# Powers of a diagonal state-space layer at half width, with the input side's table in PSUM and its products on VectorE

## The chip, the core and the metric

One core of a Trainium2 chip runs the kernel. The metric is the device time of one execution in microseconds. The engines have a queue each: TensorE (PE, matrix products), VectorE (DVE) and GpSimd (POOL) for elementwise work, ScalarE (ACT, activations and copies), and SyncE (SP), which starts the transfers. DVE, ACT and POOL read and write SBUF; PE writes PSUM, DVE and ACT read and write it too.

## The reference

The trunk maps x, one sequence of 512 rows with 1024 columns in fp32, to the same shape: an S5 state-space layer, an MLP, a dilated attention layer that reads shared keys and values, another MLP, and a last norm. Each sub-layer is an RMS norm, a shift and scale from a conditioning vector, the mixer, a gate and a residual sum. Only the state-space mixer is touched:

```python
lam_bar = jnp.exp(lam * dt)
b_bar = ((lam_bar - 1.0) / lam)[..., None] * b_mat
bu = jnp.einsum('bsgc,gpc->bsgp', ug, b_bar)
a = jnp.broadcast_to(lam_bar, (1, seq) + lam_bar.shape)
_, state = lax.associative_scan(combine, (a, bu), axis=1)
y = jnp.einsum('bsgp,gcp->bsgc', state, c_mat).real.reshape(bsz, seq, dm)
y = y + d_skip.astype(f32) * uf
z = jax.nn.gelu(y).astype(u.dtype)
val, gate = jnp.split(z @ w_glu, 2, axis=-1)
return val * jax.nn.sigmoid(gate)
```

Here `lam_bar` is a complex number for each of 64 groups and 64 states; a group has 16 input and 16 output columns.

## The kernel before

The state-space layer works in chunks of 8 steps. The 64 groups are cut into four units, `ft` = 0 to 3, and a unit into two halves, `s` = 0 and 1, of 8 groups. `ssm_powers` builds the powers of lambda by doubling, each step a complex product of six instructions (`cmul`, L352 to L357): those for b (`pcr`, `pci`) on DVE, those for c (`pwr`, `pwi`) on POOL. They are 64 groups wide on all 128 partitions (real and imaginary rows, 64 each), each with all groups.

For every unit and half, `ssm_p` makes P, powers times `bT`, by two products and a sum of 128x1024 (L562, L563, L564). `ssm_p_tr` transposes P on PE (L575), and ACT copies the result out of PSUM (L576). `ssm_q` on POOL makes Q, powers times c (L590 to L592), and small parts (L601 to L607) from which PE makes the kernel K inside a chunk (L623 to L629, copied by ACT in L642). `ssm_in_tr` turns x (L327), `ssm_in` scales and shifts it (L347, L348, or L342 on ACT). `ssm_d` multiplies it by the turned P (L665), giving each chunk's state. `ssm_scan` turns the states by the rotation angles and runs the scan on DVE (L681 to L704). `ssm_out` gives y of the unit (L718, L722, copied by ACT in L724), and `ssm_out_tr` turns it (L738), applies Gelu (L741) and casts it (L744). The GLU's matrix products are L827 to L829; their fp32 weights are split before into two parts by L799 and L801 on ACT, DVE and POOL.

Ahead of all this `norm_x` sums the squares of x on ACT (L203) and takes the root (L208); DVE makes the reciprocal `rs` (L1610), with which ACT scales x (L215). The rotation angles come from DVE (L528 to L530) and ACT (L536 to L539). `ada_steps` are the gate's parts (PE L1578, DVE L1582 and L1585).

PE, ACT, DVE and POOL run the block in the order in which `ssm` is written (the work of `ssm_params` ahead of the powers is scheduled freely). Tiles of PSUM come from two rings of four, `mm` and `aux`, of one 512-element bank each; a tile can be written when the one four places ahead of it in its ring has been read.

Of the kernel before, what the change touches and what calls it, by code (L numbers as in the profile page):

```python
# [94 lines left out]
class Trunk:  # L95
# [469 lines left out]

    def ssm_p_tr(self, ft, s):
# [5 lines left out]
        for hb in (2 * s, 2 * s + 1):  # L572
            pt = self.aux_ps().rearrange("p (g x) -> p g x", g=4)
            for j in range(4):
                nc.tensor.transpose(pt[:, j], u["pp"][:, hb * 4 + j].rearrange("p l c -> p (l c)"), self.ident)  # L575
            nc.scalar.copy(u["pT"][:, hb * 4:hb * 4 + 4], pt)  # L576

    def ssm_q(self, ft, eng):
# [16 lines left out]
        for s in range(2):
            g = s * GI + ft * 8
            g8 = slice(s * 8, s * 8 + 8)
            b8 = bz[:, 0:512].rearrange("p (g x) -> p g x", x=32)[:, g8, 16:32]
            tb = fl[:, 896:1024].rearrange("p (g c) -> p g c", c=16)
            c0 = [self.pw[4 + i][:, g:g + 8].unsqueeze(2).broadcast_to([P, 8, 16]) for i in range(2)]  # L600
            eng.tensor_tensor(b8, c0[0], self.bT[:, 0, g:g + 8], ALU.mult)  # L601
            eng.tensor_tensor(tb, c0[1], self.bT[:, 1, g:g + 8], ALU.mult)
            eng.tensor_tensor(b8, b8, tb, ALU.add)
# [1 line left out]
        for s in range(2):
            g = s * GI + ft * 8
            eng.tensor_tensor(dk[:, s * 8:s * 8 + 8], self.dT[:, g:g + 8].unsqueeze(2).broadcast_to([32, 8, 32]),  # L607
                              self.cst[0:32, C_DK:C_DK + 32].unsqueeze(1).broadcast_to([32, 8, 32]), ALU.mult)

# [1174 lines left out]
```

## Time and profile before

| what | value |
|---|---|
| time, median of three runs | 1554.1 us (1552.74 to 1558.91) |
| profiled execution | 1553.38 us, its span 1551.6 us |
| PE | busy for 1460.4 us, 94% of the span |
| DVE | 943.8 us, 61% |
| ACT | 569.1 us, 37% |
| POOL | 134.1 us, 9% |
| granted clock of PE, mean | 0.98 |

The span is the time from the first to the last instruction of the profiled execution, and the 1.8 us between it and that execution's own time lie around it. A busy share is an average over the whole span: PE's 94% are made of stretches with nearly all of it and of a beginning with much less.

### The profile page before, as it was taken

The numbers are of one execution on the slowest core, as the hardware profiler recorded it, in microseconds if no ns is written. First come the engines' busy times: TensorE is split into PE (matmuls) and PEld (weight loads), VectorE is DVE, ScalarE is ACT, GpSimd is POOL, SyncE is SP. The second block draws the span as 40 slices with busy tenths as digits, with TensorE's granted clock in tenths as the row PEclk, the third lists the DMA queues.
The fourth block names the chain that finished last, engine by engine and source line by source line (L and its number), as shares of the span: only waits on it lengthen the run. The fifth ranks groups of instructions, "written<-read, shape, count | busy, mean of one in ns | idle before, by whom it ended". The sixth has DMA issues, their size and how long they took to land.

```text
span 1551.6 us, 27063 instructions
## 1 busy us (share of the span) xinstructions
PE 1460.4 (94%) x11540; PEld 1224.5 (79%) x11540; DVE 943.8 (61%) x1641; ACT 569.1 (37%) x989; POOL 134.1 (9%) x112
## 2 busy tenths in 40 slices
PE   2666999999999999999999999999999999999998
PEld 1445789888888888987987888898779888888887
DVE  8999996889984345626646756533558434344322
ACT  5556633423242233522323322332435413232222
POOL 8867100000000000100000000000000000000000
PEclk9788999999999999999999999999999999999999
DMA  9413580976643333233444445222324233232301
GB/s 225 140 56 83 163 245 28 309 233 213 205 151 109 109 99 111 65 99 116 137 130 137 144 115 151 83 56 72 122 83 136 82 109 105 85 109 82 109 1 55
DMA packets 214488, 188.59 MB, mean 122 GB/s; under 512 B 7480, under 2 KB 208352, under 8 KB 214368
## 3 DMA queue, kind: packets, MB, share of 16 engines
q1 hardware_dynamic: 214368, 186.87, 39.5%
q8 instruction: 90, 1.47, 0.4%
q14 instruction: 30, 0.25, 0.1%
HBM read 182.66 MB, written 4.19 MB: 120 GB/s over the span
## 4 chain that ended last, share of the span: by engine, by line
PE 82%; DVE 12%; DMA 2%; issue 2%; ACT 1%; SPq 0%; POOL 0%; DVEq 0%; ACTq 0%
PE mm L827 22%; PE mm L828 22%; PE mm L829 22%; PE mm L1253 2%; PE mm L1254 2%; PE mm L1255 2%; DVE W L801 1%; PE mm L1170 1%; DMA h<-in_ada_w_dram 1%; PE aux L1107 1%; PE aux L1142 1%; PE mm L1163 1%; DVE W L563 1%; PE aux L1115 1%; DVE aacc L1495 1%
## 5 line engine op out<-in xcount | busy, mean ns | idle before, releaser
L799 ACT CAST W<-W 128x1024 fp32r<-128x1024 f32 (+1 forms) x228 | 223.7, 1031 | 392.2 <-PE mm L828 202.0
L827 PE MATMUL mm<-uz,W 128*128 128x512 f32 (+1 forms) x952 | 360.2, 381 | 2.9 <-DVE h L1385 2.7
L829 PE MATMUL mm<-uz,W 128*128 128x512 f32 (+1 forms) x952 | 358.6, 377 | 3.0 <-DVE W L801 3.0
L828 PE MATMUL mm<-uz,W 128*128 128x512 f32 (+1 forms) x952 | 358.3, 377 | 2.5 <-DVE uz L749 2.1
L801 DVE TENSOR_TENSOR W<-W,W 128x1024 fp32r<-128x1024 f32 (+1 forms) x228 | 266.3, 1196 | 148.3 <-ACT W L799 123.1
L827 PE MATMUL mm<-hid,W 128*128 128x512 f32 (+1 forms) x792 | 298.5, 378 | 0.6 <-ACT W L1277 0.3
L828 PE MATMUL mm<-hid,W 128*128 128x512 f32 (+1 forms) x792 | 296.1, 374 | 2.7 <-DVE hid L1001 2.7
L829 PE MATMUL mm<-hid,W 128*128 128x512 f32 (+1 forms) x792 | 295.5, 373 | 0.0
L827 PEld LDWEIGHTS mm<-uz,W 128*128 128x128 f32 x952 | 180.1, 189 | 36.9 <-DVE h L1385 2.8
L829 PEld LDWEIGHTS mm<-uz,W 128*128 128x128 f32 x952 | 180.2, 189 | 35.9 <-DVE W L801 3.4
L828 PEld LDWEIGHTS mm<-uz,W 128*128 128x128 f32 x952 | 180.1, 189 | 34.6 <-DVE uz L749 2.6
L828 PEld LDWEIGHTS mm<-hid,W 128*128 128x128 f32 x792 | 149.2, 188 | 29.4 <-DVE hid L1001 3.8
L827 PEld LDWEIGHTS mm<-hid,W 128*128 128x128 f32 x792 | 148.8, 188 | 28.4 <-issue 1.4
L829 PEld LDWEIGHTS mm<-hid,W 128*128 128x128 f32 x792 | 149.0, 188 | 26.5
L852 DVE SCALAR_TENSOR_TENSOR h<-mm,ada,h 128x512 f32<-128x512 f32 (+1 forms) x77 | 54.1, 707 | 150.7 <-PE mm L829 150.6
L1495 DVE SCALAR_TENSOR_TENSOR aacc<-W,cs,aacc 128x256 f32<-128x256 f32 x196 | 95.3, 486 | 4.0
L1029 DVE TENSOR_TENSOR sg<-sg 128x512 f32<-128x512 f32 x64 | 43.7, 687 | 56.4 <-ACT uz L1028 56.2
L1027 ACT ACTIVATE sg<-mm 128x512 f32<-128x512 f32 x60 | 35.6, 595 | 115.5 <-PE mm L829 114.0
L1253 PE MATMUL mm<-W,hid 128*128 128x256 f32 x256 | 73.5, 287 | 0.0
L1254 PE MATMUL mm<-W,hid 128*128 128x256 f32 x256 | 72.4, 283 | 0.0
L1255 PE MATMUL mm<-W,hid 128*128 128x256 f32 x256 | 72.4, 283 | 0.0
L1126 ACT ACTIVATE sg<-aux,st 128x192 f32<-128x192 f32 (+3 forms) x64 | 36.7, 577 | 95.4 <-DVE st L1124 95.4
(329 smaller groups left out, 1694.5 us busy)
## 6 DMA issues: line engine op xcount, KB each, us to landing
W<-in_mlp_w_dram SPq DMA_DIRECT2D x64, 1024.0 KB, 5.4
W<-in_ada_w_dram SPq DMA_DIRECT2D x20, 1024.0 KB, 7.3
h<-in_ada_w_dram SPq DMA_DIRECT2D x64, 256.0 KB, 3.1
W<-in_w_kv_dram SPq DMA_DIRECT2D x12, 1024.0 KB, 5.3
W<-in_w_kv_dram SPq DMA_DIRECT2D x24, 512.0 KB, 4.3
W<-in_attn_w_q_dram SPq DMA_DIRECT2D x24, 512.0 KB, 5.9
W<-in_ssm_w_glu_dram SPq DMA_DIRECT2D x16, 512.0 KB, 5.4
W<-in_kv_ada_w_dram SPq DMA_DIRECT2D x8, 1024.0 KB, 5.5
```

The costliest lines, as they stand in the source:

```text
L799: h = (nc.gpsimd.tensor_copy if first else nc.scalar.copy)(wh[:, ks], raw[:, ks])
L801: j = eng.tensor_tensor(wl[:, ks], raw[:, ks], wh[:, ks].bitcast(F32), ALU.subtract)
L827: nc.tensor.matmul(o, wh[:, k], uh, start=(start and k == order[0]), stop=False)
L828: nc.tensor.matmul(o, wh[:, k], ul, start=False, stop=False)
L829: self.pe_mark = nc.tensor.matmul(o, wl[:, k], uh, start=False, stop=(stop and k == order[-1])).ins
L852: self.mark = nc.vector.scalar_tensor_tensor(self.h[k][:, cs], src[:, cs], gate[:, k:k + 1], self.h[k][:, cs], ALU.mult, ALU.add).ins
L1029: nc.vector.tensor_tensor(rl, rl, rl, ALU.mult)
L1126: self.act_mark = nc.scalar.activation(p[:, 0:W], ps[:, 0:W], AF.Exp, bias=st[:, 1, e:e + 1], scale=0.125, accum_out=st[:, 2, e:e + 1]).ins
L1253: nc.tensor.matmul(ps[:, j], us[0], wh, start=(k == 0), stop=False)
L1254: nc.tensor.matmul(ps[:, j], us[0], wl, start=False, stop=False)
L1255: nc.tensor.matmul(ps[:, j], us[1], wh, start=False, stop=(k == KT - 1))
L1495: i = nc.vector.scalar_tensor_tensor(acc, raw[k], self.cs[:, k:k + 1], acc, ALU.mult, ALU.add)
```

## The change

The q vectors (lambda, its eighth power's angle and size, and the factor of b) are no longer doubled. Twelve small products with the identity (`by_set`) put the two halves of the groups on two sets of 64 partitions, so the powers are 32 wide instead of 64 on the same 128 partitions. DVE's 24 instructions of `cmul` fall from 64, 64, 128 and 256 elements to half of that, and POOL's 18 from 64, 128 and 192.

From there the powers are spread out again by ACT. Those for c go to an SBUF table by four copies of 64x512. Those for b go to a tile of PSUM, `pcu`, which is held for the whole block: `ssm_pc(ft)` copies one unit's part with eight copies of 64x64, into one of two halves of the tile in turn. It is called for unit 0 in `ssm_powers` and for the others ahead of their P.

P is made on DVE alone. Its products read `pcu`. The products of P(1,1) leave POOL, and P(2,1) is no longer divided between DVE and POOL. For units 0 and 1 the sum is not made on DVE: PE adds the two products, with two products by the identity into the same part of PSUM in place of one transpose. Units 2 and 3 keep sum and transpose. In `ssm_q` three instructions take the place of six, and one the place of two. The reciprocal `rs` moves ahead of P(0,0). `d0` and `d1`, two tiles of the `aux` ring before, share one. Lines behind L417 have other numbers than before.

```diff
+    def by_set(self, out, x):
+
+        for s in range(2):
+            rows = slice(s * GI, s * GI + GI)
+            self.nc.tensor.matmul(out[s * 64:s * 64 + 64], x[rows], self.ident[rows, rows], start=True, stop=True,
+                                  tile_position=(s * GI, s * 64))
+
...
-        G = 64
+        G = GI
...
-            nc.tensor.transpose(pt[:, i], q[:, i].rearrange("g s n -> g (s n)"), self.ident[0:G, 0:G])
-        pw = self.w([P, 4, 8, G])
-        pwr, pwi, pcr, pci = [pw[:, i] for i in range(4)]
-        t1, t2, t3, t4 = [qx[:, 16 + 4 * i:20 + 4 * i] for i in range(4)]
+            self.by_set(pt[:, i], q[:, i])
+
+        pw = self.w([P, 48, G])
+        self.pw = pw[:, 0:32].rearrange("p (i l s) g -> p i l s g", i=2, s=2)
+        pcr, pci = self.pc = [pw[:, 32 + 8 * i:40 + 8 * i] for i in range(2)]
+        pws = qx[:, 0:8].rearrange("p x (y g) -> p (x y) g", y=2).rearrange("p (i l) g -> p i l g", i=2)
+        pwr, pwi = pws[:, 0], pws[:, 1]
+        t1, t2, t3, t4 = [qx[:, 16 + 4 * i:20 + 4 * i, 0:G] for i in range(4)]
...
-        self.pw = (pwr, pwi, pcr, pci, pc0[:, 0], pc0[:, 1])
+        self.pcu = self.aux_ps().rearrange("p (b x) -> p b x", b=2)
+        self.ssm_pc(0)
+        for c in range(2):
+            for s in range(2):
+                nc.scalar.copy(self.pw[c * 64:c * 64 + 64, :, :, s], pws[s * 64:s * 64 + 64])
+
+    def ssm_pc(self, ft):
+
+        pc = self.pcu[:, ft % 2].rearrange("p (i l s g) -> p i l s g", i=2, s=2, g=8)
+        for c in range(2):
+            for s in range(2):
+                for i in range(2):
+                    self.nc.scalar.copy(pc[c * 64:c * 64 + 64, i, :, s],
+                                        self.pc[i][s * 64:s * 64 + 64, :, ft * 8:ft * 8 + 8])
 
     def ssm_turns(self):
 
@@ -539,8 +558,12 @@
         act(er, er, AF.Sin, scale=-TWO_PI, bias=self.half_pi)
 
     def pw4(self, i, ft, s, n):
-        g = s * GI + ft * 8
-        return self.pw[i][:, 0:n, g:g + 8].rearrange("p l g -> p g l").unsqueeze(3).broadcast_to([P, 8, n, 16])
+        g = slice(ft * 8, ft * 8 + 8)
+        if i < 2:
+            x = self.pw[:, i, 0:n, s, g]
+        else:
+            x = self.pcu[:, ft % 2].rearrange("p (i l s g) -> p i l s g", i=2, s=2, g=8)[:, i - 2, 0:n, s]
+        return x.rearrange("p l g -> p g l").unsqueeze(3).broadcast_to([P, 8, n, 16])
...
-            pp, tp = u["pp"][:, s * 8 + g.start:s * 8 + g.stop], tz[:, g]
-            pr, pi, b1, b2 = [x[:, g] for x in (self.pw4(2, ft, s, 8), self.pw4(3, ft, s, 8),
-                                               self.ch4(self.bT, 0, ft, s, 8), self.ch4(self.bT, 1, ft, s, 8))]
-            eng.tensor_tensor(pp, pr, b1, ALU.mult)
-            eng.tensor_tensor(tp, pi, b2, ALU.mult)
+        pp = u["pp"][:, s * 8:s * 8 + 8]
+        tp = u["zs"][:, 2 * s:2 * s + 2].rearrange("p i g c -> p (i g c)").rearrange("p (g l c) -> p g l c", g=8, c=16)
+        eng.tensor_tensor(pp, self.pw4(2, ft, s, 8), self.ch4(self.bT, 0, ft, s, 8), ALU.mult)
+        eng.tensor_tensor(tp, self.pw4(3, ft, s, 8), self.ch4(self.bT, 1, ft, s, 8), ALU.mult)
+        u["p", s] = [pp]
+        if ft < 2:
+            u["p", s].append(tp)
+        else:
             eng.tensor_tensor(pp, pp, tp, ALU.add)
 
     def ssm_p_tr(self, ft, s):
@@ -572,7 +596,12 @@
         for hb in (2 * s, 2 * s + 1):
             pt = self.aux_ps().rearrange("p (g x) -> p g x", g=4)
             for j in range(4):
-                nc.tensor.transpose(pt[:, j], u["pp"][:, hb * 4 + j].rearrange("p l c -> p (l c)"), self.ident)
+                xs = [x[:, hb % 2 * 4 + j].rearrange("p l c -> p (l c)") for x in u["p", s]]
+                if len(xs) == 1:
+                    nc.tensor.transpose(pt[:, j], xs[0], self.ident)
+                    continue
+                for k, x in enumerate(xs):
+                    nc.tensor.matmul(pt[:, j], x, self.ident, start=(k == 0), stop=(k == 1))
             nc.scalar.copy(u["pT"][:, hb * 4:hb * 4 + 4], pt)
...
+        c0 = [self.pw[:, i, 7, :, g].unsqueeze(3).broadcast_to([P, 2, 8, 16]) for i in range(2)]
+        bs = [self.bT[:, i].rearrange("p (s g) c -> p s g c", s=2)[:, :, g] for i in range(2)]
+        eng.tensor_tensor(b8, c0[0], bs[0], ALU.mult)
+        eng.tensor_tensor(tb, c0[1], bs[1], ALU.mult)
+        eng.tensor_tensor(b8, b8, tb, ALU.add)
...
-        d0, d1 = self.aux_ps(), self.aux_ps()
+        d01 = self.aux_ps()
+        d0, d1 = d01[:, 0:P], d01[:, P:]
...
+        self.nc.vector.reciprocal(self.rs, self.rs)
         self.ssm_p(0, 0, dve)
-        self.nc.vector.reciprocal(self.rs, self.rs)
         self.scale_x(0)
...
         self.ssm_p_tiles(1)
-        self.ssm_p(1, 1, pool)
+        self.ssm_pc(1)
+        self.ssm_p(1, 1, dve)
         self.ssm_q(1, pool)
...
         self.ssm_p_tiles(2)
+        self.ssm_pc(2)
         self.ssm_p(2, 0, dve)
...
-        self.ssm_p(2, 1, dve, pool)
+        self.ssm_p(2, 1, dve)
         self.ssm_q(3, pool)
...
         self.ssm_p_tiles(3)
+        self.ssm_pc(3)
         self.ssm_p(3, 0, dve)
         self.ssm_p_tr(3, 0)
         self.some(steps, 1)
```

In `order` rows, the number behind a name tells tiles of one name apart, and xN stands for N instructions in a row. First DVE's queue at the end of the powers, where `rs` is the norm's reciprocal and `W_365`, `W_366` are the products of P of unit 0. Before:

```order
L562 TENSOR_TENSOR W_365<-W_290,W_156 128x1024
L563 TENSOR_TENSOR W_366<-W_290,W_156 128x1024
L564 TENSOR_TENSOR W_365<-W_365,W_366 128x1024
L1610 RECIPROCAL rs_363<-rs_363 128x8
L528 TENSOR_TENSOR hid_468<-cst_63,rq_294 128x2048
L529 TENSOR_SCALAR hid_469<-hid_468 128x2048
L530 SCALAR_TENSOR_TENSOR hid_468<-hid_469,hid_468 128x2048
L293 TENSOR_TENSOR sg_473<-aux_281,cst_63 128x128
```

After, with `W_382` and `W_383` as these products and `aux_343` as `pcu`:

```order
L357 TENSOR_TENSOR W_295<-W_295,W_121 128x128
L1638 RECIPROCAL rs_380<-rs_380 128x8
L582 TENSOR_TENSOR W_382<-aux_343,W_156 128x1024
L583 TENSOR_TENSOR W_383<-aux_343,W_156 128x1024
L547 TENSOR_TENSOR hid_488<-cst_63,rq_299 128x2048
L548 TENSOR_SCALAR hid_489<-hid_488 128x2048
L549 SCALAR_TENSOR_TENSOR hid_488<-hid_489,hid_488 128x2048
L293 TENSOR_TENSOR sg_493<-aux_281,cst_63 128x128
L295 TENSOR_REDUCE red_89_495<-sg_493 128x8
L305 TENSOR_TENSOR redb_91_501<-red_89_495,cst_63 128x16 x2
```

The reciprocal, which reads ACT's square root, has moved ahead of P(0,0) and the three rotation steps, and P's sum is gone.

Next DVE's queue between the modulation of unit 0 (L314) and scan(0), after the change (the one before has L347 in place of the first two rows of `W_568` and `W_569`, which are P of unit 1):

```order
L314 COPY mod_92_505<-aux_497 128x48
L315 SCALAR_TENSOR_TENSOR mod_92_505<-mod_92_505 128x16
L681 MEMSET sqs_512 128x8
L582 TENSOR_TENSOR W_568<-aux_343,W_156 128x1024
L583 TENSOR_TENSOR W_569<-aux_343,W_156 128x1024
L347 TENSOR_TENSOR W_384<-mm_478,mod_92_505 128x512
L348 TENSOR_TENSOR W_384<-W_384,mod_92_505 128x512
L347 TENSOR_TENSOR W_384<-mm_483,mod_92_505 128x512
L348 TENSOR_TENSOR W_384<-W_384,mod_92_505 128x512
```

Two rows of P(1,1) now stand ahead of the input of unit 0 (L347).

ACT's queue at the end of the b and c copies, before:

```order
L478 COPY W_157<-aux_195 64x64x8 x2
L203 ACTIVATE sqs_340,ss_339<-hid_93 128x512 x4
L178 COPY vcol_65_347<-aux_345 128x64
L178 COPY vcol_67_351<-aux_349 128x96
L237 COPY dT_355<-aux_353 32x64
```

and after, L537 being `ssm_pc(0)` and L529 the copies of the powers for c:

```order
L475 COPY W_157<-aux_195 64x64x8 x2
L537 COPY aux_343<-W_295 64x8x8 x8
L529 COPY W_295<-W_121 64x16x32 x4
L203 ACTIVATE sqs_357,ss_356<-hid_93 128x512 x4
L178 COPY vcol_65_364<-aux_362 128x64
L178 COPY vcol_67_368<-aux_366 128x96
```

Twelve copies have come ahead of the norm's squares.

Last, ACT's queue at `ssm_out_tr(0)` and the y copies of out(1), before:

```order
L741 ACTIVATE W_367<-aux_1117 128x4x64 x2
L741 ACTIVATE W_367<-aux_1124 128x4x64 x2
L744 CAST uz_170_1131<-W_367 128x512 x2
L724 COPY W_542<-aux_1170 128x8x64
L724 COPY W_542<-aux_1188 128x8x64
L576 COPY W_1211<-aux_1212 128x512
L576 COPY W_1211<-aux_1218 128x512
```

and after (L769 and L772 are L741 and L744 before, L752 is L724, L605 is L576):

```order
L670 COPY W_111<-aux_1045 32x4x32 x4
L769 ACTIVATE W_384<-aux_1159 128x4x64 x2
L769 ACTIVATE W_384<-aux_1166 128x4x64 x2
L772 CAST uz_170_1173<-W_384 128x512 x2
L752 COPY W_569<-aux_1212 128x8x64
L752 COPY W_569<-aux_1230 128x8x64
L537 COPY aux_343<-W_295 64x8x8 x8
L605 COPY W_1261<-aux_1262 128x512
```

The eight copies of `ssm_pc(3)`, which P(3,0) reads, stand behind the two y copies of out(1).

## Rows read from the trace of the kernel before

**Rows 1.** View by windows: stretch, length, busy time and count per engine, clock, DMA.
```profile
120.00:166.00 46.00, 36.25 (x532) 30.43 (x532) 45.38 (x52) 37.25 (x89) 28.31 (x20) 0.86 0.34 93
150.00:166.00 16.00, 12.51 (x102) 9.83 (x100) 15.72 (x22) 15.72 (x37) 6.88 (x5) 0.89 0.47 133
166.00:175.00 9.00, 7.41 (x60) 6.32 (x62) 8.79 (x17) 3.61 (x9) 0.00 (x0) 0.81 0.85 231
175.00:340.00 165.00, 165.00 (x914) 142.37 (x911) 138.26 (x264) 63.92 (x95) 2.72 (x2) 1.00 0.65 199
```

**Rows 2.** Chain that ended last, 0 to 180 us: start, length, what.
```profile
43.24 7.12 DVE hid L530
...
70.49 3.65 PE aux L575 x16
```

**Rows 3.** Timeline of DVE from 14 to 36 us: start, length, instruction, [idle before].
```profile
15.71 0.35 DVE L353 TENSOR_TENSOR W<-W 128x64 f32<-128x64 f32 x1
...
20.68 0.68 DVE L353 TENSOR_TENSOR W<-W 128x128 f32<-128x128 f32 x1
...
22.46 1.88 DVE L356 TENSOR_TENSOR W<-W,W 128x128 f32<-128x128 f32 x1
...
35.25 1.42 DVE L562 TENSOR_TENSOR W<-W,W 128x1024 f32<-128x1024 f32 x1
```

**Rows 4.** Timeline of POOL in the same stretch.
```profile
22.36 1.84 POOL L590 TENSOR_TENSOR uz<-W,W 128x896 f32<-128x896 f32 x1
```

**Rows 5.** Timeline of ACT, 8 to 56 us.
```profile
18.20 0.63 ACT L203 ACTIVATE sqs<-hid 128x512 f32<-128x512 f32 x1
...
23.57 0.59 ACT L178 COPY vcol<-aux 128x64 f32<-128x64 f32 x2 [2.39 <-PE aux L176]
...
28.54 0.27 ACT L208 ACTIVATE rs<-aux,eps 128x8 f32<-128x8 f32 x1
39.55 3.30 ACT L215 ACTIVATE W<-hid,rs 128x256 f32<-128x256 f32 x8 [10.74 <-DVE rs L1610]
...
44.18 0.48 ACT L251 COPY lam<-aux 32x64 f32<-32x64 f32 x3 [1.14 <-PE aux L247]
```

**Rows 6.** Timeline of DVE, 36 to 137 us.
```profile
55.00 2.81 DVE L564 TENSOR_TENSOR W<-W,W 128x1024 f32<-128x1024 f32 x1
...
61.72 3.15 DVE L562 TENSOR_TENSOR W<-W,W 128x1024 f32<-128x1024 f32 x1
...
84.82 1.22 DVE L562 TENSOR_TENSOR W<-W,W 128x1024 f32<-128x1024 f32 x1
...
94.58 0.68 DVE L685 TENSOR_TENSOR sg<-mm,hid 128x512 f32<-128x512 f32 x1
95.18 1.98 DVE L686 TENSOR_TENSOR W<-W,sg 128x512 f32<-128x512 f32 x1
...
122.25 2.82 DVE L562 TENSOR_TENSOR W<-W,W 128x1024 f32<-128x1024 f32 x1
...
136.68 0.68 DVE L681 TENSOR_TENSOR W<-mm,hid 128x512 f32<-128x512 f32 x1
```

**Rows 7.** Timeline of POOL, 88 to 125 us.
```profile
94.51 2.09 POOL L592 TENSOR_TENSOR uz<-uz,hid 128x896 f32<-128x896 f32 x1
```

**Rows 8.** Timeline of ACT, 56 to 137 us.
```profile
58.67 1.07 ACT L576 COPY W<-aux 128x512 f32<-128x512 f32 x2 [6.37 <-PE aux L575]
...
68.09 0.20 ACT L859 ACTIVATE scrap<-eps 128x1 f32<-128x1 f32 x1
...
76.04 7.69 ACT L229 COPY h<-mm 128x256 f32<-128x256 f32 x16 [1.28 <-PE mm L226]
...
127.99 2.03 ACT L741 ACTIVATE W<-aux 128x256 f32<-128x256 f32 x4
```

**Rows 9.** Timeline of PE, 126 to 182 us.
```profile
131.35 0.69 PE L718 MATMUL aux<-W,W 128*64 128x128 f32 x4 [5.95 <-DVE sg L1582]
...
167.59 0.79 PE L829 MATMUL mm<-uz,W 128*128 128x512 f32 x1 [2.96 <-DVE W L801]
```

More of the change, by code (lines that the diff above doesn't have):

```diff
@@ L413, in ssm_params @@
         qx = self.w([P, 32, G])
-        q = qx[0:G, 0:12].rearrange("p (i j) n -> p i j n", j=2)
+        q = qx[0:G, 0:6]
         (LR, LI, Y8, R8, CR, CI) = [q[:, i] for i in range(6)]
@@ L417, in ssm_params @@
         (RD, TH, X0, X1, X2, X3, RR, C0, S0, X4) = [x[:, i] for i in range(10)]
-        def two(y):
-            return y.unsqueeze(1).broadcast_to([G, 2, G])
         v.tensor_scalar(RD, lre, ld, None, ALU.mult)
@@ L423, in ssm_params @@
         nc.scalar.activation(RR, RD, AF.Exp)
-        nc.scalar.activation(R8, two(RD), AF.Exp, scale=float(L))
+        nc.scalar.activation(R8, RD, AF.Exp, scale=float(L))
         v.tensor_scalar(X0, TH, 1.0 / (2.0 * math.pi), MAGIC, ALU.mult, ALU.add)
@@ L437, in ssm_params @@
         v.scalar_tensor_tensor(X0, X4, -PI_4_2, X0, ALU.mult, ALU.add)
-        v.tensor_scalar(Y8, two(X0), 4.0 / math.pi, None, ALU.mult)
+        v.tensor_scalar(Y8, X0, 4.0 / math.pi, None, ALU.mult)
         v.tensor_tensor(X2, lre, lre, ALU.mult)
@@ L445, in ssm_params @@
         v.tensor_scalar(C0, X1, -2.0, 1.0, ALU.mult, ALU.add)
-        v.tensor_tensor(LR, two(RR), two(C0), ALU.mult)
-        v.tensor_tensor(LI, two(RR), two(S0), ALU.mult)
-        l1, l2 = LR[:, 0], LI[:, 0]
+        v.tensor_tensor(LR, RR, C0, ALU.mult)
+        v.tensor_tensor(LI, RR, S0, ALU.mult)
+        l1, l2 = LR, LI
         v.tensor_scalar(X0, l1, -1.0, None, ALU.add)
@@ L453, in ssm_params @@
         v.tensor_tensor(X1, X1, X3, ALU.add)
-        v.tensor_tensor(CR, two(X1), two(X2), ALU.mult)
+        v.tensor_tensor(CR, X1, X2, ALU.mult)
         v.tensor_tensor(X1, l2, lre, ALU.mult)
@@ L457, in ssm_params @@
         v.tensor_tensor(X1, X1, X3, ALU.subtract)
-        v.tensor_tensor(CI, two(X1), two(X2), ALU.mult)
+        v.tensor_tensor(CI, X1, X2, ALU.mult)
         bc = [self.w([P, 2, G, 16]) for _ in range(2)]
@@ L488, in ssm_powers @@
         pool = nc.gpsimd
-        G = 64
+        G = GI
         q, qx = self.q, self.qx
-        pt = self.aux_ps().rearrange("p (i g) -> p i g", g=G)
+        pt = self.aux_ps()[:, 0:6 * G].rearrange("p (i g) -> p i g", g=G)
         for i in range(6):
-            nc.tensor.transpose(pt[:, i], q[:, i].rearrange("g s n -> g (s n)"), self.ident[0:G, 0:G])
-        pw = self.w([P, 4, 8, G])
-        pwr, pwi, pcr, pci = [pw[:, i] for i in range(4)]
-        t1, t2, t3, t4 = [qx[:, 16 + 4 * i:20 + 4 * i] for i in range(4)]
+            self.by_set(pt[:, i], q[:, i])
[5 more added lines that the diff above has]
+        t1, t2, t3, t4 = [qx[:, 16 + 4 * i:20 + 4 * i, 0:G] for i in range(4)]
         v.tensor_copy(pwr[:, 0], pt[:, 0])
         v.tensor_copy(pwi[:, 0], pt[:, 1])
-        pc0 = pw[:, 0:2, 7]
+        pc0 = pws[:, :, 7]
         v.tensor_copy(pc0, pt[:, 4:6])
         rq = self.t([P, 2, GI], "rq")
-        for s in range(2):
-            rows = slice(s * 64, s * 64 + 64)
-            v.tensor_copy(rq[rows], pt[rows, 2:4, s * GI:(s + 1) * GI])
+        v.tensor_copy(rq, pt[:, 2:4])
         self.y8, self.r8 = rq[:, 0], rq[:, 1]
@@ L552, in ssm_p_tiles, with ssm_p @@
         u["zs"] = self.w([P, 4, 8, NC])
-    def ssm_p(self, ft, s, eng, eng2=None):
+    def ssm_p(self, ft, s, eng):
         u = self.unit[ft]
-        tz = u["zs"][:, 2 * s:2 * s + 2].rearrange("p i g c -> p (i g c)").rearrange("p (g l c) -> p g l c", g=8, c=16)
-        for eng, g in ((eng, slice(0, 5)), (eng2, slice(5, 8))) if eng2 else ((eng, slice(0, 8)),):
-            pp, tp = u["pp"][:, s * 8 + g.start:s * 8 + g.stop], tz[:, g]
-            pr, pi, b1, b2 = [x[:, g] for x in (self.pw4(2, ft, s, 8), self.pw4(3, ft, s, 8),
-                                               self.ch4(self.bT, 0, ft, s, 8), self.ch4(self.bT, 1, ft, s, 8))]
-            eng.tensor_tensor(pp, pr, b1, ALU.mult)
-            eng.tensor_tensor(tp, pi, b2, ALU.mult)
+        pp = u["pp"][:, s * 8:s * 8 + 8]
[6 more added lines that the diff above has]
+        else:
             eng.tensor_tensor(pp, pp, tp, ALU.add)
@@ L594, in ssm_q @@
         bz = u["bz"] = self.bz[ft % 2]
[L595 to L603, printed above, removed]
+        b8 = bz[:, 0:512].rearrange("p (s g x) -> p s g x", s=2, x=32)[:, :, :, 16:32]
+        tb = fl[:, 0:256].rearrange("p (s g c) -> p s g c", s=2, c=16)
+        g = slice(ft * 8, ft * 8 + 8)
+        c0 = [self.pw[:, i, 7, :, g].unsqueeze(3).broadcast_to([P, 2, 8, 16]) for i in range(2)]
[3 more added lines that the diff above has]
+        eng.tensor_tensor(b8, b8, tb, ALU.add)
         dk = u["dk"] = self.t([32, 16, 32], "rstd", 2)
[L605 to L608, printed above, removed]
+        d = self.dT.rearrange("p (s f j) -> p f s j", s=2, j=8)[:, ft]
+        eng.tensor_tensor(dk.rearrange("p (s j) x -> p s j x", s=2), d.unsqueeze(3).broadcast_to([32, 2, 8, 32]),
+                          self.cst[0:32, C_DK:C_DK + 32].unsqueeze(1).unsqueeze(1).broadcast_to([32, 2, 8, 32]),
+                          ALU.mult)
     def ssm_k(self, ft):
```

## The prediction, before the changed kernel ran

> **What bounds the kernel now.** I read the view by windows first. From 175 us on TensorE (PE) is busy in every microsecond and the clock is at its upper level [rows 1]; VectorE (DVE) is the second there, at 138 of 165 us. The change touches nothing in that part, so it can act only by moving the moment at which PE becomes saturated. Ahead of 175 us PE has gaps: 9.8 us between 120 and 166, 1.6 us between 166 and 175, at clocks of 0.86 and 0.81 [rows 1], while DVE is busy for 45.4 of 46 us. So I read the chain next: through the SSM block it runs nearly without break over DVE, with a few pieces of PE and ACT. Two of its pieces matter later: the rotation's last step, 7.12 us for one instruction, and the transposes of P(1,0) and P(1,1), 3.65 us for 16 [rows 2]. The last long gap of PE is at 167.59, behind a weight split on DVE that stands after the last scan [rows 9]. What the change is worth is therefore the time at which DVE finishes its four scans, less what PE can fill in.
>
> Why is DVE slow? The timelines show instructions that wait, not work. A 128x128 product of the powers takes 0.68 us, and 1.88 us when a 128x896 product of POOL begins 0.1 us ahead of it [rows 3, 4]. The products of P take 1.22 us each with POOL idle, 2.81 to 3.15 us beside it [rows 6]. A DVE instruction with one operand in PSUM does not wait: 0.68 us at 94.58, while the very next one, with two SBUF operands, needs 1.98 us, both beside POOL's 2.09 us [rows 6, 7].
>
> **The change, step by step**, on the clock of the profiled execution.
>
> 1. *Powers.* DVE's 24 products become 32, 32, 64 and 128 wide. From the starts in [rows 3] a 64-wide one costs 0.28 us and a 128-wide one about 0.6; with 0.25 for 32: 12 x 0.25 + 6 x 0.35 + 6 x 0.55 = 8.4 at most, about 7 where POOL is out of the way. POOL's first Q product now waits for ACT's copies of the powers, which stand behind the end of the powers, so nothing of POOL but its own narrow powers runs beside them. From 15.5 that ends at 22 to 24 (22.7 taken), against 35.25 [rows 3]: **-12.5**.
> 2. *ACT's queue.* The eight copies of pc(0) and four of the powers stand ahead of the norm's squares (the order rows show it). For an ACT copy of 64 elements the nearest rows are 0.48/3 = 0.16 us (64 elements) and, above it, 3.30/8 = 0.41 (256 elements) [rows 5]; I take 0.2, near the first, so 1.6 for eight, from 1.3 to 3.3. The four wide ones are like L178's 0.59 [rows 5]: 2.4. Thus 22.7 + 1.6 + 2.4 = 26.7. The squares up to the square root took 18.20 to 28.81, with 2.39 of it waiting [rows 5]: 8.2 of work. So rs is ready at 34.9. Before, it was ready at 28.8 and nobody on DVE waited. The reciprocal now stands ahead of P(0,0), so P(0,0), two rotation steps and all behind wait for it: **+12.5**, and P(0,0) starts at 35 as before. Scaling x starts at 35.2 instead of 39.55 [rows 5].
> 3. *P(0,0), rotation, P(0,1).* Two products instead of three, 2.4 instead of 4.1. POOL has only Q(0) from about 27 to 41 and no P, so the rotation's last step costs about 2.4 (twice a 1024-wide product) instead of 7.12; P(0,1) costs 2.4 instead of the 5.2 that end at 57.8 [rows 6]. Sum -1.7 - 4.7 - 2.8 = -9.2: DVE is through P(0,1) at about 48.
> 4. *P(1,1) moves to DVE, ahead of the first input product,* and reads pc(1). Its copies stand in ACT's queue behind P_tr(0,1)'s copies, which waited for PE until 58.67, the rotation's Abs and Sin, the scaling of x and a table load, which ran without a gap from 58.67 to 68.29 [rows 8]: 9.6 us. P_tr(0,1) has 32 instructions of 0.11 to 0.23 (half and whole of 3.65/16 [rows 2]) instead of 8, so its first copy starts at 50 to 52. Then 51 + 9.6 + 1.6 = 62. DVE stands still for **14 us**; behind the waiting P(1,1) stand the input of unit 0, P(1,0), scan(0), and PE's P_tr(1). With 2.4 + 3.2 + 2.4 the scan starts at 70, as it did. What the head gained is spent here: **0**.
> 5. *P_tr(1).* 64 instructions instead of 16 [rows 2]: 6.8 at full clock to 14.6 at half, so 3.2 to 11 more. Behind them PE turns x for the residual, ACT copies it (7.69 us [rows 8]), and pc(2) stands behind these copies. P(2,0) itself was uncontended already (1.22 [rows 6]) and is now 4 to 11 late at its start. Some of this falls into the time that DVE waits for PE ahead of scan(1). I take **+3.5** at scan(1), from +1 to +8.
> 6. *P(2,1) whole on DVE,* products from PSUM, its add still beside POOL: 4.2 instead of 6.1: **-1.9**.
> 7. *P(3,0)* reads pc(3), which stands behind the y copies of out(1). In ACT's queue: 12 K copies, the Gelu of unit 0 from 127.99 [rows 8], shifted by +1.6 and half done about 130.6; then out(1) on PE, 6 us at the pace of its first four (0.43 from start to start, 131.35 on [rows 9]) or half of that at full clock; then 0.6 and 1.6 of copies. P(3,0) starts at 136 to 139, against 122.25 [rows 6]. Before, it was the other way round: out(1) waited 5.95 us for DVE's gate step, which stands behind P(3,0) [rows 9]. But Q(3) is over by then: P(3,0), the gate step and P(3,1) take 3.6 + 1.6 + 3.6 instead of the 14.4 from 122.25 to scan(2) at 136.68 [rows 6]. Scan(2) starts at 145.8: **+9**, from +5.5 to +11.
> 8. *What PE makes of it.* The weight split behind scan(3) is 9 late and PE's wait of 167.59 with it. Of the 16 and 9 us ahead, PE was idle for 3.49 and 1.59 [rows 1], and GLU products of units 0 and 1, which hang on none of this, lie in its queue. If they fill these 5.1 us, **+3.9** remain.
>
> The doubled q vectors, two fewer DVE copies and POOL's shorter Q cost or save some tenths under the waits of steps 2 and 4: nothing, as long as these waits are there, and up to -2 without them. The profiled execution took 1553.4, so 1557.3; the median of the runs is 0.7 above it. I say 1557.
>
> [...]
>
> [...]
>
> **Rivals.** (a) *The waits stay short: faster.* If ACT's queue is passed sooner (pc copies at 0.16, PE at full clock, P_tr(0,1) hardly longer), the 9 us of step 3 reach scan(1), and out(1) at full clock puts P(3,0) at the low end. Then scan(2) stands at -9 - 1.9 + 5.5 or about -5 to -9, and PE's wait at 167.59 shrinks by as much: 1545 to 1549. For it: ACT is idle for 10.74 and 6.37 us in the head [rows 5, 8]. Against it: these gaps are waits for DVE and PE, which remain. It decides from about 10 us less at P(1,1). Chance 0.23. (b) *The waits on ACT go through to the end: slower.* PE with longer gaps runs at half clock, steps 5 and 7 come out at their upper ends (+11 at scan(2)), and PE can't fill because its queue is in program order and out(2) stands ahead of the GLU products: +9 to +14, 1562 to 1568. For it: the clock was 0.81 to 0.89 in [rows 1] with shorter gaps. Against: the GLU products of units 0 and 1 that follow out(2). Chance 0.27. (c) *A PSUM operand does not help:* P waits for POOL as before. P(1,0), P(1,1) and P(2,1), beside Q, then cost 2.8 per product instead of 1.2, six of them or 9.6 us, on top of the forecast's 3.9 as far as PE can't fill it: +8 to +13, 1562 to 1567. The row at 94.58 speaks against it. Chance 0.08.
>
> **How the numbers follow.** My forecast has 0.42. A measurement of this kernel tells about 0.5%, 7.8 us, from no change: below 1546.3 faster, above 1561.9 slower. Of (a) 0.2 falls in faster and the rest in same; (b) and (c) are slower, 0.35; with the edges of the forecast itself (1553 to 1562) that leaves 0.45 for the same. The range reaches from within (a), 1547, to (b)'s upper half, 1568; the forecast's own is 1553 to 1562.
>
> **What would show it.** Right: DVE's powers end at 22 to 24 us; DVE idle about 12 us ahead of the reciprocal, 14 ahead of P(1,1), over 10 ahead of P(3,0), released by ACT each time; products of P at 1.2 us beside POOL; P_tr(1) at 7 us or more; scan(2) 5 us or more late. Wrong: a P(1,1) that starts before 55, P(3,0) before 130, or P's products over 2 us beside POOL. The prediction falls if PE is saturated well before 175, or after 184.

## The result, and the profile after

The changed kernel took 1563.9 us in the median of five runs (1561.5 to 1565.5), the kernel before 1556.4 in the five that were timed beside it: a ratio of 1.0054, 95% interval 1.0042 to 1.0066. So it is slower by about half a percent, 7.4 us by the medians and 9.5 us by the spans of the profiled executions (1561.1 against 1551.6). The time lies in the range that was given, and the interval of the ratio takes in the 0.5% that was set between "the same" and "slower".

The view by windows of the changed kernel answers to [rows 1]:

```profile
120.00:166.00 46.00, 27.95 (x447) 23.30 (x449) 27.53 (x39) 26.38 (x68) 16.76 (x13) 0.72 0.26 70
166.00:175.00 9.00, 9.00 (x79) 8.16 (x76) 8.94 (x10) 8.80 (x22) 6.16 (x4) 0.76 0.35 111
175.00:340.00 165.00, 165.00 (x943) 142.72 (x942) 144.58 (x272) 69.84 (x108) 3.91 (x3) 1.00 0.67 204
```

PE is busy in all of the stretch from 166 us on already, but it had less done by then: 27.95 us busy between 120 and 166 instead of 36.25, at a clock of 0.72 instead of 0.86.

DVE's timeline of the changed kernel answers to [rows 3] and [rows 6]; L582 and L583 are P's products, L588 its sum, L709 the first step of a scan, L829 the weight splits behind the last scan:

```profile
21.09 0.28 DVE L357 TENSOR_TENSOR W<-W,W 128x128 f32<-128x128 f32 x1
33.55 0.20 DVE L1638 RECIPROCAL rs<-rs 128x8 f32<-128x8 f32 x1 [12.19 <-ACT rs L208]
33.67 1.17 DVE L582 TENSOR_TENSOR W<-aux,W 128x1024 f32<-128x1024 f32 x1
...
40.28 2.59 DVE L549 SCALAR_TENSOR_TENSOR hid<-hid,hid 128x2048 f32<-128x2048 f32 x1
...
62.20 1.23 DVE L582 TENSOR_TENSOR W<-aux,W 128x1024 f32<-128x1024 f32 x1 [14.25 <-ACT aux L537]
...
69.39 0.68 DVE L709 TENSOR_TENSOR W<-mm,hid 128x512 f32<-128x512 f32 x1
...
90.99 1.22 DVE L582 TENSOR_TENSOR W<-aux,W 128x1024 f32<-128x1024 f32 x1 [8.63 <-ACT aux L537]
...
93.38 2.64 DVE L588 TENSOR_TENSOR W<-W,W 128x1024 f32<-128x1024 f32 x1
...
102.54 0.69 DVE L709 TENSOR_TENSOR W<-mm,hid 128x512 f32<-128x512 f32 x1 [2.17 <-PE mm L693]
...
116.81 1.22 DVE L582 TENSOR_TENSOR W<-aux,W 128x1024 f32<-128x1024 f32 x1
...
119.20 2.09 DVE L588 TENSOR_TENSOR W<-W,W 128x1024 f32<-128x1024 f32 x1
...
141.78 1.23 DVE L582 TENSOR_TENSOR W<-aux,W 128x1024 f32<-128x1024 f32 x1 [18.00 <-ACT aux L537]
...
150.03 0.68 DVE L709 TENSOR_TENSOR W<-mm,hid 128x512 f32<-128x512 f32 x1
...
178.99 8.29 DVE L829 TENSOR_TENSOR W<-W,W 128x512 fp32r<-128x512 f32 x10
```

ACT's timeline has the copies; L537 are those of the table for b (`pc`), L529 those for c:

```profile
21.25 1.91 ACT L537 COPY aux<-W 64x64 f32<-64x64 f32 x8 [3.18 <-DVE W L356]
23.18 2.52 ACT L529 COPY W<-W 64x512 f32<-64x512 f32 x4
...
33.25 0.27 ACT L208 ACTIVATE rs<-aux,eps 128x8 f32<-128x8 f32 x1
...
60.25 1.91 ACT L537 COPY aux<-W 64x64 f32<-64x64 f32 x8
...
89.04 1.91 ACT L537 COPY aux<-W 64x64 f32<-64x64 f32 x8
...
139.84 1.91 ACT L537 COPY aux<-W 64x64 f32<-64x64 f32 x8
```

The four waits in brackets on DVE (12.19, 14.25, 8.63 and 18.00 us) are what the reader is to see, each ended by ACT, and each, but for the first, by the last of eight copies that stand right ahead in ACT's rows. DVE's busy time between 120 and 166 fell from 45.4 to 27.5 us, as the wait of 18.00 us ahead of P(3,0) lies in that stretch. The product at 116.81 takes 1.22 us although POOL's is running, as the timeline of POOL has it:

```profile
116.20 2.25 POOL L619 TENSOR_TENSOR uz<-W,W 128x896 f32<-128x896 f32 x1 [4.66 <-PE aux L1606]
```

One thing that the prediction did not see is on PE. There L604 is P_tr(1), L601 P_tr(2,1), L766 out_tr(0), L693 d(2), and L746 the first of out(1):

```profile
72.69 7.41 PE L604 MATMUL aux<-cst,W 128*128 128x128 f32 x64
...
123.20 1.12 PE L601 MATMUL aux<-cst,W 128*128 128x128 f32 x4 [0.68 <-ACT W L605]
124.99 1.12 PE L766 MATMUL aux<-cst,W 128*128 128x128 f32 x4 [0.68 <-ACT W L605]
130.41 1.12 PE L766 MATMUL aux<-cst,W 128*128 128x128 f32 x4 [4.30 <-ACT W L670]
131.46 3.69 PE L693 MATMUL mm<-hid,W 128*64 128x64 f32 x64
134.93 0.64 PE L746 MATMUL aux<-W,W 128*64 128x128 f32 x4
```

Before, the same three stood without a gap:

```profile
119.96 1.94 PE L575 MATMUL aux<-cst,W 128*128 128x128 f32 x8 [12.57 <-DVE sqs L653]
121.72 1.66 PE L738 MATMUL aux<-cst,W 128*128 128x128 f32 x8
123.31 2.09 PE L665 MATMUL mm<-hid,W 128*64 128x64 f32 x64
```

The second half of out_tr(0) starts 5.4 us after the first one, released by ACT's copies of K, and d(2) stands at 131.46 instead of 123.31. The PSUM table keeps one of the four tiles of the `aux` ring, so the transposes have to wait for each other's copies; e7 below tests this by itself.

### The profile page after: what moved, and what is told of

It is laid out like the page before. It is cut to its first block, busy times and chain, and to the rows that moved or that the text cites. A ratio compares the mean times of both kernels' runs of the same rounds, so it can differ in the third digit from the quotient of the medians.

```text
span 1561.1 us, 27299 instructions
## 1 busy us (share of the span) xinstructions
PE 1471.0 (94%) x11654; PEld 1239.1 (79%) x11654; DVE 904.3 (58%) x1639; ACT 579.8 (37%) x1025; POOL 103.0 (7%) x90
## 4 chain that ended last, share of the span: by engine, by line
PE 83%; DVE 8%; ACT 4%; DMA 3%; issue 2%; SPq 0%; DVEq 0%; ACTq 0%
PE mm L855 22%; PE mm L856 22%; PE mm L857 22%; PE mm L1281 2%; PE mm L1282 2%; PE mm L1283 2%; DVE W L829 1%; PE mm L1198 1%; PE aux L604 1%; DMA W<-in_mlp_w_dram 1%; PE aux L1135 1%; DMA h<-in_ada_w_dram 1%; PE aux L1170 1%; PE mm L1191 1%; PE aux L1143 1%
## 5 line engine op out<-in xcount | busy, mean ns | idle before, releaser
L829 DVE TENSOR_TENSOR W<-W,W 128x1024 fp32r<-128x1024 f32 (+1 forms) x228 | 268.6, 1206 | 149.5 <-ACT W L827 125.4
```

The source lines that it names most:

```text
L829: j = eng.tensor_tensor(wl[:, ks], raw[:, ks], wh[:, ks].bitcast(F32), ALU.subtract)
```

## The experiments

Each ratio is against runs of the kernel before that were timed beside that variant.

**e1: each unit's copies one unit earlier.**

```diff
         self.scale_x(0)
+        self.ssm_pc(1)
...
-        self.ssm_pc(1)
+        self.ssm_pc(2)
         self.ssm_p(1, 1, dve)
...
-        self.ssm_pc(2)
+        self.ssm_pc(3)
         self.ssm_p(2, 0, dve)
...
-        self.ssm_pc(3)
         self.ssm_p(3, 0, dve)
```

> The changed kernel with each unit's eight copies to PSUM made one unit earlier in ScalarE's order (unit 1 behind the first scaling of x, unit 2 where unit 1's stood, unit 3 where unit 2's stood); nothing else differs. Theory: VectorE stood still for 14.3, 8.6 and 18.0 us ahead of P(1,1), P(2,0) and P(3,0) only because of where these copies stand. Then P(1,1) starts at about 48 instead of 62, P(3,0) within 3 us of the end of unit 2's input, scan(2) at 125 to 135 instead of 150, and the time is 1543 to 1551, below the kernel before. Rival one (PE's doubled instructions in P_tr and their half clock hold the scans back) and rival two (one tile fewer in the aux ring, since the PSUM table keeps one, holds out(1) back): the waits only move to PE, scan(2) not before 143, time 1557 or more.

Measured: 1.0057 (1.0036 to 1.0077), no faster than the changed kernel. The theory's numbers were missed, but the edit had not done what it was meant to. DVE's timeline of e1:

```profile
65.03 1.22 DVE L582 TENSOR_TENSOR W<-aux,W 128x1024 f32<-128x1024 f32 x1 [16.49 <-ACT aux L537]
...
134.90 1.22 DVE L583 TENSOR_TENSOR W<-aux,W 128x1024 f32<-128x1024 f32 x1 [6.05 <-PE aux L766]
```

P(1,1) waited until 65.03 for the eight copies of unit 2 (63.10 to 65.00 on ACT), which now stand ahead of it in the program: a product waits for the last write to the table's tile, not to its half. At P(3,0) the wait for copies is gone; its second product waits 6.05 us for PE's out_tr(0) instead, which frees its tile. That is the second rival's place.

**e2: the table for b in SBUF, spread once.**

```diff
+        self.pcw = pw[:, 32:64].rearrange("p (i l s) g -> p i l s g", i=2, s=2)
...
-        self.pcu = self.aux_ps().rearrange("p (b x) -> p b x", b=2)
-        self.ssm_pc(0)
-        for c in range(2):
-            for s in range(2):
-                nc.scalar.copy(self.pw[c * 64:c * 64 + 64, :, :, s], pws[s * 64:s * 64 + 64])
+        for dst, src in ((self.pcw, pcs), (self.pw, pws)):
+            for c in range(2):
+                for s in range(2):
+                    nc.scalar.copy(dst[c * 64:c * 64 + 64, :, :, s], src[s * 64:s * 64 + 64])
```

> The changed kernel with the b powers spread once, behind the powers, by four copies of 64x512 to a table in SBUF as those for c are; no PSUM table, no later copies, four tiles in the aux ring again. Theory: the waits ahead of P(1,1), P(2,0) and P(3,0) vanish as in e1, but P's products beside Q take 2 us and more again: 1547 to 1555. Rival two: most of the gain comes from the ring, so this one is as fast as e1 or faster, and the stretch from P_tr(2,1) to out(1) on PE is 4 us shorter than in e1. If a PSUM operand gave nothing, e2 would be faster than e1.

Measured: 0.9970 (0.9960 to 0.9980), 1550.2 us: 13 us below the changed kernel, and below the kernel before. DVE's timeline shows P(2,1), with both operands in SBUF, at 2.72 and 3.09 us instead of 1.22 each, and hardly a wait ahead of P(3,0), at 122.76; scan(2) starts at 131.75:

```profile
113.35 2.72 DVE L583 TENSOR_TENSOR W<-W,W 128x1024 f32<-128x1024 f32 x1
115.99 3.09 DVE L584 TENSOR_TENSOR W<-W,W 128x1024 f32<-128x1024 f32 x1
...
122.76 1.71 DVE L583 TENSOR_TENSOR W<-W,W 128x1024 f32<-128x1024 f32 x1 [0.29 <-PE aux L602]
...
131.75 0.68 DVE L710 TENSOR_TENSOR W<-mm,hid 128x512 f32<-128x512 f32 x1
```

On PE out_tr(0) runs in one piece again and d(2) stands at 124.45:

```profile
122.55 1.97 PE L767 MATMUL aux<-cst,W 128*128 128x128 f32 x8
124.45 2.77 PE L694 MATMUL mm<-hid,W 128*64 128x64 f32 x64
```

**e3: P's sum on DVE for all units; e4: the reciprocal behind P(0,0).**

```diff
-        if ft < 2:
-            u["p", s].append(tp)
-        else:
-            eng.tensor_tensor(pp, pp, tp, ALU.add)
+        eng.tensor_tensor(pp, pp, tp, ALU.add)
```

> The changed kernel with P's sum on VectorE and a transpose for units 0 and 1 too (as units 2 and 3 have it), all else as changed. Theory: PE loses about 8 us of instructions ahead of 80 us, VectorE gets four sums of 1.2 to 2.6 us, all in or ahead of stretches in which it waits for the copies: the time moves by less than 3 us from 1564. Rival one: PE's doubled P_tr is the cause, and the time falls to 1559 or below, P(2,0) starting 4 us or more earlier.

```diff
-        self.nc.vector.reciprocal(self.rs, self.rs)
         self.ssm_p(0, 0, dve)
+        self.nc.vector.reciprocal(self.rs, self.rs)
```

> The changed kernel with the reciprocal rs behind P(0,0) again, as before the change. Theory: P(0,0) starts at about 23.3 instead of 33.7, but the rotation still waits for rs at 33.6, so everything behind is 2.3 us earlier at most and the wait ahead of P(1,1), which ScalarE ends, keeps 12 us or more: 1561 to 1564. A rival that lays the loss on the moved reciprocal would want 10 us back: 1554.

Measured: 1.0061 (1.0035 to 1.0088) and 1.0047 (1.0029 to 1.0064). Neither can be told from the changed kernel. In e3 scan(2) starts 3.5 us earlier (146.5) and the span is 0.4 us shorter; in e4 P(0,0) starts at 23.45 and the product of P(1,1) at 62.38, as before that edit. So giving back P_tr's added instructions (64 in the trace for P_tr(1) instead of 16), at the price of four sums on DVE, wins nothing here, and the moved reciprocal is not the cause of the loss.

**e5: copies behind the last reader of the table.** Unit 1's stand where e1 had them, unit 2's behind P(1,0), unit 3's behind P(2,1):

```diff
         self.ssm_p(1, 0, dve)
+        self.ssm_pc(2)
...
         self.ssm_p(2, 1, dve)
+        self.ssm_pc(3)
```

> The changed kernel with each unit's eight copies to the PSUM table right behind the last product that reads the table ahead of them in the program (unit 1 behind the first scaling of x, unit 2 behind P(1,0), unit 3 behind P(2,1)). In e1 VectorE's P(1,1) still waited for the copies of unit 2, which stood ahead of it, since a product waits for the last write to the table's tile, whichever half. Theory: now P(1,1) starts at 48 to 50, scan(0) at 56 to 60 instead of 69, scan(2) at 130 or earlier, time 1545 to 1552, as e2. Rival two (the aux ring with a tile less): the head gains 10 us or more up to scan(0), but PE's d(2) and out(1) still stand 6 us or more behind P_tr(2,1) because out_tr(0)'s second half waits for the K copies; e5 ends 3 to 8 us behind e2, 1552 to 1559.

Measured: 1.0014 (1.0002 to 1.0026), as the second rival had it. DVE's waits for the table's copies are gone; scan(0) starts at 59.2 and scan(1) at 87.0. P(3,0) waits again, and for PE (L601 is P_tr(2,1)):

```profile
112.88 1.23 DVE L582 TENSOR_TENSOR W<-aux,W 128x1024 f32<-128x1024 f32 x1
114.02 1.22 DVE L583 TENSOR_TENSOR W<-aux,W 128x1024 f32<-128x1024 f32 x1
...
123.73 1.22 DVE L582 TENSOR_TENSOR W<-aux,W 128x1024 f32<-128x1024 f32 x1 [4.36 <-PE aux L601]
...
132.78 0.69 DVE L709 TENSOR_TENSOR W<-mm,hid 128x512 f32<-128x512 f32 x1 [0.72 <-PE mm L693]
```

**e7: e2 with three tiles in the ring.** One tile is taken and held, and nothing else is changed:

```diff
+        self.held = self.aux_ps()
+        nc.scalar.copy(self.held[0:1, 0:1], rq[0:1, 0, 0:1])
...
         self.ssm_p(3, 1, dve)
+        scrap = self.t([1, 8], "scrap2")
+        act(scrap[:, 0:1], self.held[0:1, 0:1])
```

> e2 (table in SBUF, written once) with one tile of the aux ring taken behind the powers, written by one copy of one element, and read again by one element behind P(3,1), so that the ring has three tiles through the block as with the PSUM table; nothing else. Rival two: P_tr's copies wait for PE one by one, out_tr(0)'s second half waits for the K copies, and the time goes up by 3 to 8 us from e2: 1553 to 1558. Theory (the waits for the copies are all of it): within 2 us of e2, 1548 to 1552.

Measured: 1.0007 (0.9996 to 1.0019) against 0.9970 for e2, so 0.37% or 5.8 us for the tile alone. PE's timeline (L769 is out_tr(0), L696 d(2)) has the waits of the changed kernel again, 4.30 us of wait for K's copies in the middle of out_tr(0) and d(2) at 131.25:

```profile
124.79 1.12 PE L769 MATMUL aux<-cst,W 128*128 128x128 f32 x4 [0.68 <-ACT W L608]
130.21 1.12 PE L769 MATMUL aux<-cst,W 128*128 128x128 f32 x4 [4.30 <-ACT W L673]
131.25 2.93 PE L696 MATMUL mm<-hid,W 128*64 128x64 f32 x64
```

**e12 and e13: the PSUM table in the other ring.**

```diff
-        self.pcu = self.aux_ps().rearrange("p (b x) -> p b x", b=2)
+        self.pcu = self.mm_ps().rearrange("p (b x) -> p b x", b=2)
```

> e5 with the PSUM table in a tile of the other ring, mm, so that aux has its four tiles. If the short aux ring is what costs, P_tr(2,1) and out_tr(0) run in one piece again, P(3,0) does not wait for PE, and the time falls by 4 to 7 us from e5 to e2's: 1549 to 1553. If the mm ring pays the same price (its tiles carry the turned x and the chunk states), the time stays within 2 us of e5: 1556 to 1560.

> e12 with e8's two edits (four squares ahead of the copies, the reciprocal behind P(0,0)). As e8 against e2: at most 2 us less than e12, as the head is then held by ScalarE's rotation and PE; if P on PSUM operands is worth something where Q runs, it is the fastest of all, 1543 to 1547.

Measured: 1.0060 (1.0045 to 1.0075) and 1.0043 (1.0028 to 1.0058). Out_tr(0) ran in one piece in e12, but the `mm` ring pays more than `aux` did: scan(1) starts at 97.7 in e12 instead of 87.0 in e5. PE turns x for the residual through `mm` (L226), and ACT copies it (L229): in e5 these copies ran in one piece, from 73.31 to 80.97 us, and DVE waited 1.05 us for the PE step behind them (L308), until 81.03. In e12 it waited 10.33 us there, until 90.32. That PE and ACT waited for each other's tiles of `mm` in that time is an inference from the order of the kernel, as ACT's timeline of e12 is not shown. The second case of that expectation was still too mild: neither ring has a tile to spare in this block. In e13 scan(0) starts at 55.1, earlier than in all others, and scan(1) at 96.5 even so; the 1543 to 1547 hoped for there were missed.

**e8, e9: the head of e2, and the sum.** In e8 the spreading copies stand behind the first four squares, and the reciprocal behind P(0,0); e9 adds e3's edit to it.

```diff
         self.some(norm, 4)
+        self.ssm_spread()
...
-        self.nc.vector.reciprocal(self.rs, self.rs)
         self.ssm_p(0, 0, dve)
+        self.nc.vector.reciprocal(self.rs, self.rs)
```

> e2 with the first four squares of the norm ahead of the eight spreading copies on ScalarE (it waits 3 us for the powers there), and the reciprocal behind P(0,0) again. Theory: rs is ready at 31 instead of 34.2, P(0,0) stands in the time in which VectorE waits for it (done by about 30) and no longer beside Q, so the rotation starts at 31.5 to 32 instead of 39.2, scan(0) 5 to 7 us earlier than in e2, and the time is 1543 to 1548. If PE or ScalarE holds the head, scan(0) moves by less than 3 us and the time stays at 1549 to 1551.

> e8 with P's sum on VectorE and a transpose for units 0 and 1 too. With the waits for the copies gone, PE's 64 instructions of P_tr(1) and ScalarE's copies behind them (1.2 us apart) stand on the path to scan(1). If PE's doubled form costs there, scan(1) starts 2 to 4 us earlier and the time falls by 2 to 4 us from e8; if the four sums on VectorE (1.2 us, 2.6 beside Q) cost more than PE gains, it rises by 1 to 4 us.

Measured: 0.9955 (0.9939 to 0.9971) and 0.9986 (0.9977 to 0.9996). The reciprocal came at 31.65 as expected, but scan(0) did not move (63.4 against 63.1 in e2): a miss in its place, since the three rotation steps now took 10.6 us (6.9 in e2), and rows of P and of the input behind them took longer too (2.82 us at 50.19 and 1.88 at 53.65; 1.21 and 0.69 in e2). That Q's wide products on POOL are the cause is an inference from the changed kernel, where those of Q(0) ran from 25.13 to 36.54; e8's timeline of POOL is not shown. Nor can e8's time be told from e2's: the intervals overlap. DVE's timeline of e8:

```profile
31.65 0.20 DVE L1646 RECIPROCAL rs<-rs 128x8 f32<-128x8 f32 x1 [5.86 <-ACT rs L208]
31.77 3.85 DVE L553 TENSOR_TENSOR hid<-cst,rq 128x2048 f32<-128x2048 f32 x1
35.65 2.70 DVE L554 TENSOR_SCALAR hid<-hid 128x2048 f32<-128x2048 f32 x1
38.39 4.05 DVE L555 SCALAR_TENSOR_TENSOR hid<-hid,hid 128x2048 f32<-128x2048 f32 x1
...
63.43 0.68 DVE L715 TENSOR_TENSOR W<-mm,hid 128x512 f32<-128x512 f32 x1
```

e9 is slower than e8 by 0.3%: where nothing else holds DVE, P's sum is worth having on PE. In the changed kernel it was hidden (e3).

**e10, e11: the rotation first, and all sums on PE.**

```diff
+        self.ssm_turns()
         self.ssm_p_tiles(0)
...
-        self.ssm_turns()
```

> e8 with the three rotation steps on VectorE ahead of P(0,0) and the reciprocal, as they need neither. In e8 they took 10.6 us beside Q, behind a wait of 5.9 us for rs. If VectorE's queue holds the head, P(0,1) starts 8 to 10 us earlier, scan(0) at 54 to 58 instead of 63.4, and the time is 1541 to 1547; if what follows the head holds (PE ahead of scan(1), the last units' queue of ScalarE and the GLU weights), scan(2) moves by less than 3 us and the time stays within 2 us of e8.

> e10 with P's sum on PE for units 2 and 3 too, so VectorE makes only products. VectorE loses four sums of 1.2 to 2.7 us; PE gets 96 more instructions, in stretches in which it waits up to P_tr(3,0) and in a busy one behind it. If VectorE's queue decides still, 2 to 4 us below e10; if PE and its ring do, within 2 us of it or above.

Measured: 0.9943 (0.9927 to 0.9960), 1545.4 us, and 0.9938 (0.9922 to 0.9953), 1545.7 us. The rotation takes 5.8 us instead of 10.6 in DVE's timeline of e10, and scan(0) starts at 58.5:

```profile
21.44 2.28 DVE L553 TENSOR_TENSOR hid<-cst,rq 128x2048 f32<-128x2048 f32 x1
23.75 1.23 DVE L554 TENSOR_SCALAR hid<-hid 128x2048 f32<-128x2048 f32 x1
25.01 2.29 DVE L555 SCALAR_TENSOR_TENSOR hid<-hid,hid 128x2048 f32<-128x2048 f32 x1
...
58.48 0.68 DVE L715 TENSOR_TENSOR W<-mm,hid 128x512 f32<-128x512 f32 x1
```

Both are faster than the kernel before, and by about 1.1% faster than the changed one, if its 1.0054 is divided out; e11 cannot be told from e10, and neither can be told from e8 by its interval.

The starts of some steps, from the timelines of DVE and PE, with the spans (us; "last turn" is PE's first transpose of out_tr(3)):

| kernel | scan(0) | scan(1) | d(2) | scan(2) | last turn | span |
|---|---|---|---|---|---|---|
| before | 70.3 | 92.8 | 123.3 | 136.7 | 181.6 | 1551.6 |
| changed | 69.4 | 102.5 | 131.5 | 150.0 | 187.6 | 1561.1 |
| e1 | 72.2 | 105.8 | 134.7 | 142.0 | 189.3 | 1560.8 |
| e2 | 63.1 | 87.4 | 124.5 | 131.8 | 174.7 | 1546.7 |
| e5 | 59.2 | 87.0 | 130.8 | 132.8 | 183.6 | 1555.3 |
| e7 | 63.3 | 87.9 | 131.3 | 138.6 | 183.3 | 1556.3 |
| e10 | 58.5 | 83.2 | 120.2 | 127.5 | 170.4 | 1540.6 |

The span follows PE's column "last turn" within 3.5 us, and not scan(2): e5 has scan(2) 3.9 us ahead of the kernel before and the last turn 2 us behind it, with d(2) 7.5 us late.

## Why the prediction was right, and where it was not

The direction and the three waits were as forecast, the total was too small: 7.4 us by the medians instead of 3.9. The 1563.9 us lie outside the forecast's own 1553 to 1562; it is rival (b), with 1562 to 1568, that brings them into the range. By its steps:

1. *Powers*: forecast to end at 22.7, ended at 21.4, a little below the 22 to 24 that was given as a sign of being right.
2. *ACT's queue*: the reciprocal at 34.9 forecast, 33.55 measured, after a wait of 12.19 (12.5). Eight copies took 1.91 us, 0.24 each, where 0.2 was taken. e4 shows no cost of the reciprocal's new place.
3. *P(0,0), rotation, P(0,1)*: through at 46.8, 48 forecast. The last rotation step took 2.59 instead of 7.12.
4. *P(1,1)*: at 62.20 after 14.25 us of wait (62 and 14), scan(0) at 69.39 (70). Right.
5. *P_tr(1) and P(2,0)*: 7.41 us for 64 instructions at a granted clock of 1.00 (6.8 to 14.6 forecast; half the time per instruction of the row used, 3.65 us for 16 at a clock of 0.50, makes 7.3), P(2,0) 6.2 us late (4 to 11). But scan(1) came 9.8 us late, outside the +1 to +8: P(2,0) now stood at the time at which Q(2) runs (its wide products on POOL from 93.14 to 105.96), and its sum took 2.64 us instead of 1.23, the modulation's last step 1.46 instead of 0.21, and L348 of the input 1.88 instead of 0.69. The wait for PE ahead of scan(1), which was to take up some of the delay, stayed (2.17 us, 2.43 before). The step's +3.5 was mis-sized.
6. *P(2,1)*: 4.4 us instead of 6.1. Scan(1) itself ran 14.3 us, with POOL busy for 9.5 of them, instead of 20.9 with POOL busy for 20.5, which the prediction did not count. The two errors cancelled by luck: the input of unit 2 ended at 123.8, 1.5 us late, and 1.6 were forecast.
7. *P(3,0)*: forecast at 136 to 139, came at 141.78, and scan(2) at +13.4 instead of +9. This is the step that failed in its mechanism. The prediction let out(1) start when the first half of unit 0's Gelu was done, about 130.6. It started at 134.9, since d(2) stood ahead of it, held up by out_tr(0) in the ring of three, and ran slower: 3.69 us at a granted clock of 0.50 instead of 2.09 at 1.00, behind a stretch from 120 to 131 us in which PE was busy for 3.91 us. That the table holds a tile stands in the section on the change; its price was not asked for. e7 measured it at 0.37% by itself. The step's low end was also mis-added: 130.6 + 3 + 2.2 + 8.8 make 144.6, 8 us late and not 5.5, and rival (a) took the 5.5 over.
8. *What PE makes of it*: 5.1 us were to be filled in. The last turn came 6.0 us late instead of 13.4, so 7.4 were filled in up to there. But the path was another. The weight splits behind the last scan came 13.3 us late (165.66 before, 178.99 after), and PE's wait of 167.59 did not move with them, as the step had it: it was gone. PE's last wait in this part of the changed kernel was for ACT's copies of K, ahead of out(2), and from its end at 164.48 to 200 us PE stood still no more. That is 3.1 us earlier than before, with less work done by then; taken by PE's gaps, it meets the sign of falling that was named, a PE saturated well before 175.

DVE's timeline before:

```profile
165.66 6.09 DVE L801 TENSOR_TENSOR W<-W,W 128x512 fp32r<-128x512 f32 x10
```

PE's timeline after:

```profile
164.48 0.69 PE L746 MATMUL aux<-W,hid 128*64 128x128 f32 x4 [3.46 <-ACT W L670]
```

The span was 9.5 us longer, so 3.5 came back after the last turn. This may be no more than the spread of executions: those of the kernel before lie up to 6.2 us apart, and its profiled one is 3.1 below their median. What happens behind 200 us was not tried and stays open. The prediction's own sum makes 1558 (1557.3 and 0.7 for the median), where 1557 was said.

Of the rivals, (b) had the right end and half of the mechanism. The waits on ACT go through, and scan(1) and scan(2) came later still than its upper ends (9.8 and 13.4 us late, +8 and +11 forecast), with d(1) at a clock of 0.50 too (3.68 us instead of 2.08 at 1.00); but PE did fill in, which (b) had ruled out. Half of the loss against e2 is these waits (the changed kernel at 1.0054, e5 at 1.0014), half the tile (e7 against e2). (c) is out: products with a PSUM operand took 1.22 us beside POOL (116.81, with POOL's product of 2.25 us from 116.20). But this gained no time that can be told: the intervals of e5, with the table in PSUM, and e7, with the table in SBUF and the same ring, overlap. Scan(2) starts 5.8 us earlier in e5, but PE's d(2) (130.8 and 131.3) and the last turn (183.6 and 183.3) stand level in the two. (a) is what e2 and e10 have: what is left of the change brings 0.3% once ACT's repeated copies and the tile are out of the way (e2), and 0.6% with the head put in order (e10). The half-width powers were not run by themselves.
